# First layer's experts: four weight loads issued in front of the overflow branch, and the first gather of tokens moved behind its own table

## The chip, the cores and the metric

The kernel runs on one core of a Trainium2 chip. The metric is the device time of one execution in microseconds (us). A core has TensorE (PE, matmuls; PEld is its weight load), VectorE (DVE), ScalarE (ACT), GpSimd (POOL) and SyncE (SP), which here issues nearly all loads and stores. Each engine works through its own list of instructions in order and waits on semaphores for the others.

## The reference

Two layers of a diffusion backbone. Each layer modulates and normalises 256 latent and 256 context tokens of width 1024, runs four kinds of attention side by side, and then a mixture of 16 gated experts, of which each token uses two. Cut to the part that matters here:

```python
def _hier_moe(h, wg, bg, we, be, w_gate, w_up, w_down):
    lg = hf @ wg + bg;  grp = argmax(lg)            # one of 4 groups
    le = hf @ we + be                               # 16 experts, the group's 4 are looked at
    top_v, top_i = lax.top_k(le_sel, 2)             # two experts a token
    w_top = softmax(top_v) * p_grp
    for e in range(16):
        a = silu(hf @ w_gate[e]) * (hf @ w_up[e])
        y = y + gate[:, e:e + 1] * (a @ w_down[e])  # 1024 -> 512 -> 1024
```

The first layer does this for all 512 tokens, the second for the 256 latent ones. The weights of one expert are 6 MB in f32, so a layer's experts read 96 MB.

## The kernel before

`moe(l, ...)` first takes the tokens in four chunks of 128 (`for chs, xg, rg, vec in chunks`), routes them and, in the first layer, stores the modulated rows to a DRAM tile `hfD` (lines 1218, 1258 and 1269). It then sorts the tokens' choices, works out a flag (does any expert have more tokens than its slot holds?) and runs `full_experts()` in the first layer and `half_experts()` in the second.

Weights go through a ring of ten buffers of 1 MB (`RING[0]`: two of kind `ra`, eight of kind `rb`). The order of all loads is laid down in `todo`: gate 0 (two loads), then up 0, gate 1, down 0, up 1, gate 2, down 1 and so on, each in two halves. `fetch(n)` issues the next n of them on SP (the issue itself is line 1159, in `load_expert`); `weights()` issues one more whenever a load is used. The constant `FILL` says how many go out where:

```python
FILL = ((4, 1, 1, 0, 1), (10,))     # line 40; first layer, second layer
```

In the first layer four go out when the last chunk begins, one behind each of two stores of `hfD` (line 1218), `FILL[0][3]` of them behind the last store (line 1258), and `FILL[0][4]` at the top of the experts' loop. The rest of the ring is issued inside the first expert, behind its gather; `late=True` puts a one-element memset on GpSimd (line 1158) in front of the first of these. In the second layer all ten go out before the branch.

`overflow()` (lines 1821 and 1822) reads the flag on every engine and skips, by a branch that all five engines take, a block that would treat overflowing experts with loads, gathers and the same buffers. In the skipped case the engines still add to their semaphores, at the join, what the block would have added; on SP these are eight semaphore instructions, one for each counter of loads.

Behind the branch `table(i)` builds expert i's table: one-hots on VectorE (line 1450), small matmuls (line 1452), and the index of its tokens (line 1459). `sort_experts()` sorts the experts by their number of tokens. `start(i)` begins expert i's generator: a gather of 128 rows of `hfD` by GpSimd (line 1490), eight transposes (1500), a copy of their high part by ScalarE (1502) and the low part by VectorE (1503), then the split of each half-load of weights into a high part (ScalarE, line 1472) and a low part (VectorE, in some places GpSimd, line 1474), and three kinds of matmul for each piece (1483, 1484 and 1485; the last one uses the low part of the tokens, line 1503). Down weights go through lines 1533 to 1535. Seven of the 16 experts are small and use the weights directly (lines 1552 to 1596). `tc.issue_after(t[2])` in `start` puts VectorE's instructions of the block it covers behind the instruction that writes the index.

The order on each engine is not the program's: a list scheduler orders the instructions when the kernel is built, by priority in program order and by a simulated clock, except where `issue_after`, `manual_schedule` (SP's loads in the chunk loop) and `keep_in_program_order` hold it.

Of the kernel before, what the change touches and what calls it, by code (L numbers as in the profile page):

```python
# [36 lines left out]
RAW_A = 2  # L37
EB = 6
LOOK = 1
FILL = ((4, 1, 1, 0, 1), (10,))  # L40
AHEAD = 5
STEPS0 = (90, -1, 90, -2, 0, 0, 0, 0, -3, 0, 0, -4, 1, 0, 2, 3, 0, 1, 4, 5, 0, 1)
STEPS1 = (1, 6, 7, 1, 1, 8, 9, 1, 1, 1)
# [54 lines left out]
def kern(tc, I, out):  # L98
# [19 lines left out]
    def nm(s):  # L118
        cnt[0] += 1
        return f"{s}_{cnt[0]}"  # L120
# [28 lines left out]
    start = sp.tile([128, 512], F32, name=nm("amv"), tag="amv", bufs=1)  # L149
# [966 lines left out]
    def moe(l, chunks, mod2):  # L1116
# [20 lines left out]
        ring = RING[l]  # L1137
# [7 lines left out]
        def load_expert(e, n, i, late=False):  # L1145

            x = e if not isinstance(e, int) or e < nfirst else perm[e - nfirst]
            src = I[n][l, x] if isinstance(x, int) else I[n][l, ds(x, 1)].rearrange("a k n -> (a k) n")
            if n == "moe_w_down":
                src, sh = src[256 * i:256 * i + 256], [128, 2, 1024]  # L1150
            else:
                src, sh = src[512 * i:512 * i + 512], [128, 4, 512]
            src = src.rearrange("(p k) n -> p k n", p=128)
            h = sh[1] // 2
            if isinstance(e, int):
                wt = wtile(sh)
                if late:
                    tc.keep_in_program_order(G.memset(wt[0:1, 0, 0:1], 0.0))
                SY.dma_start(wt, src)
                return [wt[:, :h], wt[:, h:]]  # L1160
            ws = []
            for j in range(2):
                wt = tile4([128, h, sh[2]])
                SY.dma_start(wt, src[:, h * j:h * j + h])
                ws.append(wt)
            return ws
# [9 lines left out]
        def small_slot(e):  # L1176

            return isinstance(e, int) and e >= N_FIRST + N_BIG

        def fetch(n, late=False):  # L1180
            for i in range(min(n, len(todo))):
                k = todo.pop(0)
                ahead[k] = load_expert(*k, late and i == 0)
# [7 lines left out]
        def open_ring():  # L1191
            for kind in sorted(set(ring)):
                for i, k in enumerate(ring):
                    if k == kind:
                        first[i] = slot(k, [128, 2, 1024] if todo[i][1] == "moe_w_down" else [128, 4, 512])
# [9 lines left out]
        for chs, xg, rg, vec in chunks:  # L1205
# [4 lines left out]
            if chs[0] == 3:  # L1210
# [4 lines left out]
                loads.__enter__()  # L1215
                fetch(FILL[0][0])
                for store, i in zip(stores, FILL[0][1:]):
                    SY.dma_start(*store)
# [35 lines left out]
            if chs[0] == 3:  # L1254
# [3 lines left out]
                SY.dma_start(hfD[384:512], rg[0])  # L1258
                fetch(FILL[0][3])
                loads.__exit__(None, None, None)  # L1260
# [10 lines left out]
        if half:  # L1271
            PW = Phase(f"pw{l}", "right")
            open_ring()
            fetch(FILL[1][0])
        PX = Phase(f"px{l}")
# [152 lines left out]
        def full_experts():  # L1428
# [58 lines left out]
            def expert(tab, gi, e, xg):  # L1487
# [3 lines left out]
                                     in_offset=bass.IndirectOffsetOnAxis(ap=idx[:, gi, 0:1], axis=0),  # L1491
                                     bounds_check=N - 1, oob_is_err=False)
                if isinstance(e, int) and e == ORDER[0]:

                    fetch(len(ring) - sum(FILL[0]), True)
                Xh, Xl = [PX("t4", [128, KD, 128], F32R, bufs=T4)[:, :, :C] for _ in range(2)]
                for kp in range(2):
                    ps = tr([128, 4, 128])[:, :, :C]
# [110 lines left out]
            def more(e, rk1, rc1):  # L1609
                for _ in expert(tables(lambda i: (rk1, rc1.rearrange("p (c r) -> p c r", r=8)), 1), 0, e, xgs[0]):  # L1610
                    pass
# [4 lines left out]
            def table(i):  # L1616

                s = ORDER[i]
                if s in tabs:
                    return tabs[s]  # L1620
                if s < N_FIRST:
                    tabs[s] = tables(lambda i: (RK[:, :, s], rec[:, :, s]), 1), 0
                    return tabs[s]
                small = small_slot(s)
                end = E if small else N_FIRST + N_BIG
                n = min(3 if s in (N_FIRST, N_FIRST + N_BIG) else 4, end - s)
                rks, recs = sorted_
                t = tables(lambda i: (rks[:, :, s + i], recs[:, :, s + i]), n, small)
                tabs.update((s + i, (t, i)) for i in range(n))
                return tabs[s]  # L1630

            def start(i):
                t, gi = table(i)
                run = (small_expert if small_slot(ORDER[i]) else expert)(t, gi, ORDER[i], xgs[i % 2])
                with tc.issue_after(t[2]):
                    next(run)
                return run

            fetch(FILL[0][4])
            table(0)  # L1640
            table(1)
            rks, gw, E2s = sort_experts()
            recs = R_(E, 8, dt=BF16)
            G.tensor_copy(recs, rec)
            records(recs, E2s, gw)
            sorted_.extend((rks, recs))
            run = start(0)
            next(run)
            for i in range(E):
                if i + 2 < E:  # L1650
# [6 lines left out]
                run = then  # L1657
# [158 lines left out]
        def overflow(cols, more, before=lambda: None):  # L1816
# [5 lines left out]
            with tc.If(fv > 0):  # L1822
# [4 lines left out]
                with tc.For_i(0, E, 1) as e:  # L1827
# [5 lines left out]
                    with tc.For_i(1, N // C, 1):  # L1833
                        V.tensor_scalar(ts[0], ts[0], float(-C), None, op0=ALU.add)
                        more(e, *ts)

        acc = half_experts() if half else full_experts()


# [125 lines left out]
```

## Time and profile before

| what | us |
|---|---|
| three timed runs | 1238.98, 1249.18, 1249.64 |
| their median | 1249.18 |
| the profiled execution | 1250.01 |
| span of its core in the profile | 1248.2 |
| TensorE busy in the span | 1083.0 (87%) |
| VectorE busy in the span | 669.1 (54%) |
| ScalarE busy in the span | 465.0 (37%) |
| queue of the loads, share of the 16 DMA engines | 65.5% |

The span runs from the first to the last instruction of the core; the profiled execution's own time has 1.8 us more around it. All positions in the text are us from the span's start. Shares are averages over stages with different limits, so the stage from 380 us (end of the first layer's routing) to 700 us (end of its experts) is read by itself.

### The profile page before, as it was taken

To read this page: it belongs to the slowest core of one execution; us is meant where nothing else is said; L and a number is where in the kernel's file an instruction comes from. 1 tells how busy PE (TensorE), PEld (TensorE's weight loads), DVE (VectorE), ACT (ScalarE), POOL (GpSimd) and SP (SyncE) were. 2 spreads that over 40 slices of the span, in tenths; PEclk is the share of its full clock that TensorE was granted. 3 is DMA by queue.
4 is the path that set the end of the run, shared out by engine and by line. 5 is a ranking of instruction groups with operands and counts; after the bars stand their busy time and mean duration, and the time that the engine had idled before them with its cause. 6 is when DMAs were issued, how large, how long until landed. Compare 5 with 4: busy or idle time off the path is not lost. (4 is left out here: it accounts for less than half of the span.)

```text
span 1248.2 us, 16457 instructions
## 1 busy us (share of the span) xinstructions
PE 1083.0 (87%) x5930; PEld 689.8 (55%) x5930; DVE 669.1 (54%) x1646; ACT 465.0 (37%) x851; POOL 200.1 (16%) x218
## 2 busy tenths in 40 slices
PE   5999999979961799999989769899989699999973
PEld 2777654457751676666655347654457556565430
DVE  4377166665589795564444478636885721111103
ACT  2342155555252474444434244315563421111100
POOL 0023011212134233132221114120001000000000
PEclk9899989989985799999999978997989789989897
DMA  9843546620634799998997554543714969799995
GB/s 353 312 136 80 198 177 208 237 71 1 245 135 190 244 331 358 412 405 344 416 387 271 204 172 135 148 169 111 270 35 142 406 223 420 322 420 418 377 420 219
DMA packets 85411, 315.83 MB, mean 253 GB/s; under 512 B 20458, under 2 KB 35568, under 8 KB 55624
## 3 DMA queue, kind: packets, MB, share of 16 engines
q1 hardware_dynamic: 81340, 305.99, 65.5%
q0 software_dynamic: 3728, 8.59, 1.9%
q8 instruction: 49, 0.80, 0.3%
q14 instruction: 42, 0.34, 0.1%
q10 hardware_dynamic: 252, 0.09, 0.0%
HBM read 305.47 MB, written 13.70 MB: 256 GB/s over the span
## 5 line engine op out<-in xcount | busy, mean ns | idle before, releaser
L1474 DVE TENSOR_TENSOR hl<-rb,hl 128x1024 fp32r<-128x1024 f32 x71 | 89.1, 1280 | 49.9 <-ACT hl L1472 39.7
L1753 PE MATMUL mm<-rb,xt 128*64 128x256 f32 (+1 forms) x816 | 95.3, 405 | 4.0 <-DMA rb<-in_moe_w_up_dram 4.0
L1472 ACT ACTIVATE hl<-rb 128x1024 fp32r<-128x1024 f32 x84 | 86.1, 1054 | 31.0 <-PE mm L1484 17.6
L579 PE MATMUL mm<-s,hh 128*128 128x512 f32 x216 | 86.8, 406 | 0.0
L581 PE MATMUL mm<-s,hh 128*128 128x512 f32 x216 | 86.6, 404 | 0.0
L580 PE MATMUL mm<-s,hh 128*128 128x512 f32 x216 | 85.8, 397 | 0.0
L1753 PEld LDWEIGHTS mm<-rb,xt 128*64 128x64 f32 (+1 forms) x816 | 50.3, 133 | 39.0 <-issue 12.8
L840 ACT ACTIVATE e<-mm,nmx 128x512 f32<-128x512 f32 (+1 forms) x96 | 58.4, 616 | 29.0 <-DVE nmx L835 14.4
L1483 PE MATMUL mm<-hl,t 128*128 128x512 f32 x144 | 61.1, 424 | 4.0 <-ACT t L1502 4.0
L1485 PE MATMUL mm<-hl,t 128*128 128x512 f32 x144 | 59.2, 414 | 5.2 <-DVE t L1503 5.2
L1484 PE MATMUL mm<-hl,t 128*128 128x512 f32 x144 | 61.5, 427 | 2.3 <-DVE hl L1474 2.3
L835 DVE TENSOR_REDUCE nmx<-mm 128x1 f32<-128x512 f32 (+1 forms) x80 | 52.7, 684 | 7.3 <-PE mm L829 6.3
L849 POOL TENSOR_SCALAR e<-e,rc 128x256 f32<-128x256 f32 x32 | 30.3, 957 | 126.6 <-DVE rc L847 114.7
L440 ACT ACTIVATE s<-ra 128x1024 fp32r<-128x1024 f32 x30 | 31.3, 1055 | 50.5 <-PE mm L581 25.4
L1769 PE MATMUL mx<-rb,at 128*64 128x512 f32 (+1 forms) x192 | 45.6, 598 | 4.6 <-DMA rb<-in_moe_w_down_dram 3.1
L327 PE MATMUL mm<-ra,cT 128*32 128x512 f32 x320 | 46.0, 637 | 3.4 <-DMA ra<-in_w_ada_dram 3.4
L881 PE MATMUL tr<-cst,e 128*128 128x128 f32 x256 | 44.9, 307 | 3.9 <-DVE e L849 1.4
L1758 DVE TENSOR_TENSOR ta<-ta,mm 128x256 f32<-128x256 f32 x13 | 5.5, 420 | 79.9 <-ACT ta L1757 79.9
L579 PEld LDWEIGHTS mm<-s,hh 128*128 128x128 f32 x216 | 40.7, 189 | 12.6 <-issue 2.0
L581 PEld LDWEIGHTS mm<-s,hh 128*128 128x128 f32 x216 | 40.6, 188 | 12.2 <-issue 3.2
L881 PEld LDWEIGHTS tr<-cst,e 128*128 128x128 f32 x256 | 32.0, 154 | 27.1 <-issue 12.8
L580 PEld LDWEIGHTS mm<-s,hh 128*128 128x128 f32 x216 | 40.6, 188 | 11.4 <-issue 2.6
(552 smaller groups left out, 2341.5 us busy)
## 6 DMA issues: line engine op xcount, KB each, us to landing
rb<-in_moe_w_up_dram SPq DMA_DIRECT2D x52, 1024.0 KB
rb<-in_moe_w_down_dram SPq DMA_DIRECT2D x50, 1024.0 KB
rb<-in_moe_w_gate_dram SPq DMA_DIRECT2D x49, 1024.0 KB
ra<-in_w_ada_dram SPq DMA_DIRECT2D x40, 1024.0 KB
ra<-in_moe_w_gate_dram SPq DMA_DIRECT2D x13, 1024.0 KB
ra<-in_w_in_dram SPq DMA_DIRECT2D x24, 512.0 KB
ra<-in_moe_w_down_dram SPq DMA_DIRECT2D x11, 1024.0 KB
ra<-in_moe_w_up_dram SPq DMA_DIRECT2D x10, 1024.0 KB
```

The costliest lines, as they stand in the source:

```text
L579: T.matmul(ps, a, hi[:, k2], start=k == 0, stop=False)
L580: T.matmul(ps, a, lo[:, k2], start=False, stop=False)
L581: T.matmul(ps, b, hi[:, k2], start=False, stop=k == KD - 1)
L835: V.tensor_reduce(nmx[:, :nb], ps, axis=AX, op=ALU.max, negate=True)
L840: S.activation(e[:, b], ps[:, b], AF.Exp, bias=nmx[:, b:b + 1], accum_out=sm[:, b:b + 1])
L881: T.transpose(tp[:, k2, 128 * c:128 * c + 128], probs[hh][c][:, 0, 128 * kt:128 * kt + 128], ident)
L1472: S.activation(hi, w[k2], AF.Copy)
L1474: eng.tensor_tensor(lo, w[k2], hi.bitcast(F32), op=ALU.subtract)
L1483: T.matmul(ps[:C], ah, hs[:, k2], start=first and k2 == 0, stop=False)
L1484: T.matmul(ps[:C], ah, ls[:, k2], start=False, stop=False)
L1485: T.matmul(ps[:C], al, hs[:, k2], start=False, stop=last and k2 == 1)
L1753: T.matmul(ps[o:o + m, j], X[:, k, gi, c:c + m], wt, start=k == 0, stop=k == KD - 1)
```

## The change

The constant becomes `((4, 1, 1, 4), (10,))`: four loads behind the last store of `hfD`, none at the top of the experts' loop and none behind the gather, so that the ring's ten loads all stand before the branch. The first expert's generator now stops (`yield`) right behind its gather. `run = start(0)` moves up, between `table(0)` and `table(1)`; the rest of the first expert (transposes, copies, splits, matmuls) is traced later, by one more `next(run)` at the place where `start(0)` stood, and no longer inside the block of `issue_after`.

```diff
-FILL = ((4, 1, 1, 0, 1), (10,))
+FILL = ((4, 1, 1, 4), (10,))
...
                 if isinstance(e, int) and e == ORDER[0]:
-
-                    fetch(len(ring) - sum(FILL[0]), True)
+                    yield
                 Xh, Xl = [PX("t4", [128, KD, 128], F32R, bufs=T4)[:, :, :C] for _ in range(2)]
...
-            fetch(FILL[0][4])
             table(0)
+            run = start(0)
             table(1)
             rks, gw, E2s = sort_experts()
             recs = R_(E, 8, dt=BF16)
             G.tensor_copy(recs, rec)
             records(recs, E2s, gw)
             sorted_.extend((rks, recs))
-            run = start(0)
+            next(run)
             next(run)
             for i in range(E):
```

## Rows read from the trace of the kernel before

**Rows 1.** Busy time by stretch: us; PE, PEld, DVE, ACT, POOL; clock, DMA share, GB/s.

```profile
394.00:414.00 20.00, 6.40 (x23) 4.41 (x24) 17.94 (x64) 7.33 (x8) 6.99 (x5) 0.50 0.60 228
440.00:697.00 257.00, 241.76 (x1304) 158.96 (x1302) 140.33 (x176) 121.18 (x154) 69.96 (x43) 0.99 0.90 351
```

**Rows 2.** Waits of PE from 440 to 697 us: us in total, times, longest.

```profile
PE mm L1483 <- ACT t L1502: 2.8, 4, 2.0
...
PE mm L1570 <- ACT t L1561: 0.2, 1, 0.2
```

**Rows 3.** Waits of PE from 394 to 440 us.

```profile
PE tr L1500 <- DMA xg<-hfD,idx: 11.0, 1, 11.0
PE mm L1485 <- DVE t L1503: 3.7, 2, 2.3
```

**Rows 4.** Timeline of SP's DMA issues: start, us, engine, line, what, count.

```profile
382.34 0.78 SPq L1159 DMA_DIRECT2D rb<-in_moe_w_down_dram  x1
386.74 0.33 SPq L1258 DMA_DIRECT2D hfD<-r  x1
397.67 0.82 SPq L1159 DMA_DIRECT2D rb<-in_moe_w_up_dram  x2
400.59 0.33 SPq L1159 DMA_DIRECT2D rb<-in_moe_w_down_dram  x1
409.81 0.96 SPq L1159 DMA_DIRECT2D ra<-in_moe_w_gate_dram  x2
```

**Rows 5.** The branch's line, 380 to 400 us: ns min/median/max, first and last start.

```profile
L1822 SPq EVENT_SEMAPHORE  x8: 17/17/17, 396.7 to 397.3; - x8
...
L1822 SPq COMPARE_BRANCH  x1: 54/54/54, 393.6 to 393.6; - x1
```

**Rows 6.** Timeline of ACT, 394 to 413 us; in brackets the idle time before.

```profile
397.31 1.28 ACT L1472 ACT_TABLE_LOAD   x1 [4.95 <-SPq L1822]
398.61 3.90 ACT L1472 ACTIVATE hl<-ra 128x1024 fp32r<-128x1024 f32 x4
...
408.86 0.60 ACT L1502 ACTIVATE t<-tr 128x512 fp32r<-128x512 f32 x1 [5.40 <-PE tr L1500]
```

**Rows 7.** Timeline of DVE, 396 to 413 us.

```profile
398.04 0.22 DVE L1459 TENSOR_SCALAR idx<-tf 128x2 int32<-128x2 f32 x2
399.70 1.23 DVE L1474 TENSOR_TENSOR hl<-ra,hl 128x1024 fp32r<-128x1024 f32 x1 [1.44 <-ACT hl L1472]
...
410.00 0.87 DVE L1450 TENSOR_SCALAR oh<-cst,rt 128x128 bf16<-128x128 f32 x4
...
412.22 0.68 DVE L1503 TENSOR_TENSOR t<-tr,t 128x512 fp32r<-128x512 f32 x1
```

**Rows 8.** The gathers' line, 399 to 400 us and 430 to 435 us.

```profile
L1490 POOL DMA_INDIRECT xg<-hfD,idx x1: 1315/1315/1315, 399.2 to 399.2; - x1
...
DMA to landing us min/median/max: 8.4/8.4/8.4
...
L1490 POOL DMA_INDIRECT xg<-hfD,idx x1: 1014/1014/1014, 431.4 to 431.4; - x1
...
DMA to landing us min/median/max: 4.1/4.1/4.1
```

**Rows 9.** Busy time in stretches of 2 us; the last two columns are DMA share and GB/s.

```profile
386.00:388.00 2.00, 0.00 (x0) 0.00 (x0) 1.97 (x13) 0.21 (x1) 0.00 (x0) 0.50 1.01 410
...
392.00:394.00 2.00, 0.00 (x0) 0.00 (x0) 1.31 (x10) 0.18 (x1) 0.00 (x0) 0.50 0.00 0
...
398.00:400.00 2.00, 0.00 (x0) 0.00 (x0) 0.56 (x4) 1.99 (x3) 0.84 (x1) 0.50 0.55 160
```

**Rows 10.** The branch's line in the second layer, 985 to 1010 us.

```profile
L1822 SPq EVENT_SEMAPHORE  x8: 17/17/17, 1001.9 to 1003.6; - x8
...
L1822 SPq COMPARE_BRANCH  x1: 58/58/58, 995.9 to 995.9; - x1
```

**Rows 11.** Timeline of SP's DMA issues in the second layer, 985 to 1010 us.

```profile
986.32 0.33 SPq L1159 DMA_DIRECT2D rb<-in_moe_w_down_dram  x1
```

**Rows 12.** Busy time in a stretch of 2 us in the second layer, columns as in rows 9.

```profile
1002.00:1004.00 2.00, 2.00 (x9) 1.02 (x9) 1.03 (x5) 0.00 (x0) 0.00 (x0) 0.50 0.04 12
```

## The prediction

> **What bounds the kernel now.** The profiled execution took 1250.01 us, of which 1248.2 us are the span of its core. I read the stage that the change touches in four steps: which engine is busy, what TensorE waits for, what the waited-for engine itself waits for, and where the loads stand meanwhile.
>
> First the busy time by stage. From 440 to 697 us, the experts of the first layer, TensorE is busy 241.8 of 257 us [rows 1]. The load queues are nearly full as well (0.90), so either could be the bound; the waits decide. In those 257 us TensorE waits for other engines 15.1 us in all, spread over eleven reasons from 2.8 down to 0.2 us, and none of them is a weight load [rows 2]. So this stretch is bound by TensorE's own work, and a shift of its start goes through to the end nearly whole. From 394 to 414 us it is the other way round: TensorE is busy 6.4 of 20 us and VectorE 17.9 [rows 1]. This is where the change acts.
>
> There TensorE waits 11.0 us for the first gather, then 3.7 us in two waits for the low half of the gathered tokens (L1503, VectorE) [rows 3]. The first number looks like the prize. It isn't: after the gather TensorE can only run two of its three kinds of products. The third (L1485) needs L1503, which VectorE reaches at 412.22 [rows 7]; between 399.70 and 412.22 VectorE works without a gap on an in-order list that starts with the first low half of a weight (L1474). So the head of the stage is VectorE's list, and that list starts when ScalarE's first high half (L1472) is done.
>
> ScalarE's first work behind the branch is a table load at 397.31, after 4.95 us of idle time that SP's branch line ended [rows 6]. SP compared at 393.6, and its eight semaphore events at the join (L1822) ran from 396.7 to 397.3 [rows 5]. **SP's join at 397.3 is what releases the chain**: join, table load, L1472 at 398.61, L1474 at 399.70, L1503 at 412.22.
>
> **The change, part by part.**
>
> *Loads.* SP's list of before [rows 4] shows what the diff alone doesn't: the seventh load (down weights, 382.34) already went out in front of the branch, even ahead of the last store of tokens (386.74). Behind the branch stood three: two up loads at 397.67 and one down load at 400.59, the latter held by the small memset on GpSimd. The change issues all four behind the store at 386.74, in front of the branch. Four issues cost SP four times 0.33 to 0.41 us [rows 4], at most 1.7 us, so it is done by 388.8, long before it compares at 393.6: nothing there.
>
> When do they land? In the kernel before the queues were empty from 392 to 394 [rows 9]. Without the down load only a store (0.5 MB) and a load (1 MB), both issued before 382.34, go ahead of the last store; at the 410 GB/s of a full row [rows 9] they take 3.8 us, so they are through when it is issued. A flow begins some 1.5 us behind its issue: of the loads issued at 397.67 the row of 398 to 400 holds 0.32 MB, which at 410 GB/s is 0.8 us of transfer [rows 9]. So the store and four loads, 4.7 MB, flow from about 388.3 and need 11.5 us at 410 GB/s: until 399.8 (398.9 with 0.6 us of lag, 400.8 with 2.5 us). Then 2.5 MB are still under way when SP compares at 393.6.
>
> *The join.* In the compiled program of before each of SP's eight events first waits until all loads counted on its counter have landed, then adds what the skipped branch would have counted. At the compare of before everything had landed [rows 9], so these waits cost nothing. The second layer is the nearest row for what comes now: ten loads in front of its branch, the last issued at 986.32 [rows 11], data flowing until 1002 to 1004 [rows 12], compare at 995.9, events from 1001.9 to 1003.6 [rows 10]. The join took 7.7 us there against 3.7 here, and its last event came with the last data. So in the changed kernel the last event comes with or just behind the last load: 400.0 to 401.3, where the upper end is 393.6 plus the 7.7 us. The lower bound of the cost is nothing (if ScalarE's wait concerns only counters without a new load); I take 400.5, that is +3.2 us, as the second layer shows the very case.
>
> Of SP's 3.1 us between compare and first event [rows 5] the Trainium skill has a reason: "Runtime: NRT & Kernel Launch", section Instruction fetch mechanics, says that a taken branch to a page not at hand must wait for a DMA that fetches it. It speaks against this change, as the fetch then shares the engines with the loads; the rows agree so far (3.1 us with empty queues, 6.0 us in the second layer with full ones [rows 10]). By that rule alone the events would run from 399.6 to 400.2 and the join come +2.9 us late, which is the same story 0.3 us cheaper.
>
> *ScalarE and VectorE.* Table load, five high halves, then the copies of the gathered tokens (L1502) stand in one queue. Shifted by 3.2 us the halves run from 401.8 to about 406.6 (0.95 us apart). VectorE's first L1474 moves from 399.70 to 402.9. Everything up to L1503 stands behind it: 12.5 us of work, less what the planner may now put behind L1503. L1503 stood behind eight one-hots of the next table, two rows of 0.87 us [rows 7]; if the tokens are there sooner, these can go behind it: 0 to 1.7 us less. L1503 then starts between 413.7 and 415.4 instead of 412.22: +1.5 to +3.2 us, the middle +2.3.
>
> *The gather.* It starts at 399.2, 0.9 us behind its index (398.26), and lands 8.4 us later beside 3 MB of loads; the one at 431.4, with little beside it, took 4.1 us [rows 8]. Behind its own table alone it can hardly start sooner, as the index ends that wait already. With the loads through at 399.8 it takes 4.1 to 5 us, so the transposes start near 403.9, some 3.7 us sooner than with 8.4 us. But ScalarE is then busy with halves until 406.6; its copies start there instead of at 408.86 [rows 6], 2.3 us sooner, and L1503 waits for VectorE's list anyway. So the 3.7 us are worth nothing beyond the reordering counted above. The removed memset (under 0.1 us on GpSimd) is worth nothing.
>
> *Loads gained.* Three loads land up to 7.7 us sooner. The eleventh goes out at 409.81, when SP has read the sorted experts' numbers, and the next wait for buffers that TensorE's pace frees; TensorE waits for no load up to 697 [rows 2]. Worth nothing.
>
> **Sum.** +2.3 us at L1503, carried whole: 1250.0 + 2.3 = 1252.3 us. Its own range: 0 if the join's wait is partly empty or the two waits for L1503 (2.3 and 1.4 us) [rows 3] absorb it, +4.0 if the join ends at 401.3 and nothing is reordered.
>
> **Rivals.**
>
> *Gain.* The join's events do not hold ScalarE (its counters carry no new load), so L1474 stays at 399.70, and the earlier tokens bring L1503 up by the 1.7 us of one-hots: 1248.3. For it: ScalarE's copies could start 2.3 us sooner. Against it: the second layer's join.
>
> *Slower: the split in front of the index.* Before, VectorE's part of the first expert was traced inside the block that queues it behind the index (issue_after in start). Now that block covers the gather alone. If the planner puts one or two low halves ahead of the index, VectorE stands at 399 with the index and both tables behind a half that waits for ScalarE until 402.9 or 403.8: index at 404.6 to 405.8, gather 0.9 us later, landed at 409.6 to 410.8, which alone puts TensorE's start 2 to 3 us later; VectorE's list behind it (the 14.0 us from index to L1503 less 1.4 us of waiting [rows 7] and the half of 1.2 us that is now ahead: 11.4 us) brings L1503 to 416 to 417.2, +3.8 to +5.0: 1255. It decides as soon as one L1474 stands ahead of L1459.
>
> *Nothing moves.* The gather is ready when its index is, the seventh load was in front already, the join ends unchanged and L1503 keeps its place: 1250.0.
>
> **How the numbers follow.** Forecast (0 to +4 us) 45%; slower through the split 20%; gain 20%; nothing 15%. All four lie within 8 us. About 1% (12.5 us) is what a measurement of this kernel can tell from no change: its own three runs lie between 1238.98 and 1249.64, the median 0.8 us below the profiled execution. So the forecast is 1252. The range must hold the cases (1247 to 1256) and the scatter of a median (a run 10 us lower among three): 1240 to 1259. Faster or slower by over 1% would take a new plan of the instructions far behind the change, which no row excludes and none supports: 4% each.
>
> **What would show it.** In the profile after: four loads behind the store near 387, none from 388 to 409; SP's events at the join ending at 400.0 to 401.3; ScalarE's table load right behind them; the gather landing in 4 to 5 us; transposes near 404, yet L1503 at 413 to 415.5; the stage from 440 as busy as before. Wrong would be: events that end near 397.3 (then the gain), or L1474 ahead of L1459 (then the split).

## The result, and the profile after

The changed kernel takes 1256.76 us (median of 20 runs, 1247.74 to 1260.58) against 1248.55 us for the kernel before (20 runs, 1238.98 to 1252.03). The ratio is 1.0077, interval 1.0061 to 1.0094: 8.2 us slower by the medians, 9.6 us by the ratio. That lies inside the range of the prediction and within 1%, but 4.8 us above its number, which stood for a loss of 2.3 us. In a second set of runs the ratio was 1.009 (1.0058 to 1.0123). The profiled execution of the changed kernel took 1256.33 us, with a span of 1254.5 us. From line 1495 on, line numbers of the changed kernel are those of before minus 1 (L1501 is the old L1502, L1821 the old L1822).

The same views as before, on the changed kernel. Single executions reach the branch at different times (389 to 397 us in this study), so positions are compared by their distance from SP's compare. It is at 393.6 us before and at 392.4 us after.

SP's DMA issues (timeline), to be read against [rows 4]:

```profile
385.53 0.33 SPq L1258 DMA_DIRECT2D hfD<-r  x1
385.91 1.26 SPq L1159 DMA_DIRECT2D rb<-in_moe_w_down_dram  x2
387.21 1.02 SPq L1159 DMA_DIRECT2D rb<-in_moe_w_up_dram  x2
413.99 0.97 SPq L1159 DMA_DIRECT2D ra<-in_moe_w_gate_dram  x2
```

Four loads stand behind the last store and none until 413.99 us. The branch's line, against [rows 5]:

```profile
L1821 SPq EVENT_SEMAPHORE  x8: 17/17/17, 398.4 to 401.1; - x8
...
L1821 SPq COMPARE_BRANCH  x1: 54/54/54, 392.4 to 392.4; - x1
```

The first of the eight events comes 6.0 us behind the compare instead of 3.1, the last one 8.7 instead of 3.7. The timeline of ScalarE, GpSimd and VectorE, against [rows 6 to 8]:

```profile
398.78 1.28 ACT L1472 ACT_TABLE_LOAD   x1 [7.64 <-SPq L1821]
400.08 4.08 ACT L1472 ACTIVATE hl<-ra 128x1024 fp32r<-128x1024 f32 x4
...
415.22 0.60 ACT L1501 ACTIVATE t<-tr 128x512 fp32r<-128x512 f32 x1 [10.11 <-PE tr L1499]
...
404.29 3.30 POOL L1474 TENSOR_TENSOR hl<-ra,hl 128x1024 fp32r<-128x1024 f32 x1 [10.31 <-DVE hl L1474]
409.52 1.31 POOL L1490 DMA_INDIRECT xg<-hfD,idx  x1 [1.93 <-DVE idx L1459]
...
395.15 0.41 DVE L1376 TENSOR_TENSOR t<-rk 128x256 f32<-128x256 f32 x1
401.16 1.23 DVE L1474 TENSOR_TENSOR hl<-ra,hl 128x1024 fp32r<-128x1024 f32 x1 [5.60 <-ACT hl L1472]
...
403.04 2.35 DVE L1474 TENSOR_TENSOR hl<-ra,hl 128x1024 fp32r<-128x1024 f32 x2
...
405.45 2.42 DVE L1388 TENSOR_TENSOR t<-rk,cst 1x256 f32<-1x256 f32 x1
...
407.93 1.21 DVE L1474 TENSOR_TENSOR hl<-rb,hl 128x1024 fp32r<-128x1024 f32 x1
409.07 0.22 DVE L1459 TENSOR_SCALAR idx<-tf 128x2 int32<-128x2 f32 x2
...
415.85 0.69 DVE L1502 TENSOR_TENSOR t<-tr,t 128x512 fp32r<-128x512 f32 x1 [0.85 <-ACT t L1501]
```

This is the picture of the second rival. VectorE stands idle for 5.60 us because a low half (L1474) is now ahead of the index (L1459) and waits for ScalarE, which waits for the late join. Four low halves are ahead of the index in all. The index comes at 409.07 instead of 398.04 us, the gather at 409.52 instead of 399.2, and L1502 at 415.85 instead of 412.22. The gather itself now lands in 4.2 us instead of 8.4, which helps nobody.

Waits of TensorE from 394 to 440 us, against [rows 3], and busy time, against [rows 1]:

```profile
PE tr L1499 <- DVE rt L1417: 18.6, 1, 18.6
PE tr L1452 <- DVE oh L1450: 0.4, 1, 0.4
PE mm L1483 <- ACT t L1501: 0.3, 1, 0.3
```

```profile
394.00:414.00 20.00, 1.31 (x7) 0.73 (x7) 14.21 (x53) 6.24 (x6) 5.64 (x3) 0.50 0.29 108
...
440.00:697.00 257.00, 237.52 (x1277) 156.63 (x1278) 139.31 (x178) 119.98 (x152) 70.61 (x42) 0.99 0.91 353
```

One wait of 18.6 us takes the place of several. The 3.7 us of [rows 3] are not one place: in TensorE's timeline of the kernel before, 1.38 us of them belong to the first expert and 2.35 us to the second one, 17 us later, where 1.27 us for the high part of its tokens stand in front:

```profile
412.96 0.79 PE L1485 MATMUL mm<-hl,t 128*128 128x512 f32 x1 [1.38 <-DVE t L1503]
...
426.94 0.50 PE L1483 MATMUL mm<-hl,t 128*128 128x512 f32 x1 [1.27 <-ACT t L1502]
...
430.45 0.79 PE L1485 MATMUL mm<-hl,t 128*128 128x512 f32 x1 [2.35 <-DVE t L1503]
```

That second L1503 stands in VectorE's list of before behind one-hots of the third table and a low half:

```profile
426.51 1.95 DVE L1450 TENSOR_SCALAR oh<-cst,rt 128x128 bf16<-128x128 f32 x3
...
428.39 1.21 DVE L1474 TENSOR_TENSOR hl<-rb,hl 128x1024 fp32r<-128x1024 f32 x1
...
429.72 0.68 DVE L1503 TENSOR_TENSOR t<-tr,t 128x512 fp32r<-128x512 f32 x1
```

In the changed kernel the second stop is gone (0.3 us are left of it), and by 436 us most of the loss has disappeared. Two rows of busy time (us; PE, PEld, DVE, ACT, POOL; granted clock, DMA share, GB/s) show it, first of the kernel before, then of the changed one:

```profile
428.00:432.00 4.00, 1.65 (x5) 1.26 (x5) 3.33 (x10) 0.60 (x1) 0.57 (x1) 0.76 0.81 283
432.00:436.00 4.00, 4.00 (x18) 3.33 (x17) 0.70 (x1) 2.60 (x3) 2.84 (x2) 0.81 0.42 121
```

```profile
428.00:432.00 4.00, 3.71 (x23) 2.65 (x22) 3.69 (x9) 3.44 (x5) 2.47 (x1) 1.00 0.80 279
432.00:436.00 4.00, 4.00 (x20) 3.10 (x19) 4.00 (x8) 3.09 (x4) 2.79 (x1) 1.00 0.88 313
```

Before, after those stops, TensorE's granted clock fell from 1.00 (2.4 GHz) to 0.76 and 0.81, a mix of both levels. After, it works through at 1.00: VectorE did most of the sort and the one-hots of the second table while TensorE waited for the first gather.

All kernels of the study in one table. The times are read from their timelines: SP's compare, then the distances from it to the first L1485, to the 9th scatter and to the 15th (a scatter is the DMA by which GpSimd writes one expert's finished rows to `yD`). Behind them stands the time between these two, worked from the unrounded times. In the variants the line numbers shift by up to four; the column L1485 is the same product everywhere.

```
                            compare  L1485  9th    15th   9th-15th  median    ratio (interval)
before                      393.60   19.4   194.2  303.1  108.9     -         1
before again                392.20   19.9   195.2  304.2  109.0     -         -
changed                     392.38   25.4   195.5  308.0  112.5     1256.76   1.0077 (1.0061-1.0094)
r_after                     395.67   25.4   195.7  308.0  112.3     1260.01   1.009  (1.0058-1.0123)
e1_hold                     392.60   17.5   195.8  305.8  110.0     1252.68   1.005  (1.0031-1.007)
e2_order_only               392.66   22.7   198.4  309.7  111.2     1255.18   1.0057 (1.0028-1.0086)
e4_early                    392.97   15.4   193.7  306.0  112.3     1247.63   0.9999 (0.9975-1.0023)
n2_sort_first               392.70   19.5   194.3  306.4  112.1     1249.13   1.0024 (0.9995-1.0054)
s1_second_behind_sort       396.98   13.0   191.4  303.9  112.5     1251.02   1.0036 (1.0007-1.0065)
s2_split_behind_sort        392.83   15.4   188.2  296.9  108.8     1241.68   0.9968 (0.9942-0.9993)
r_s2                        396.22   15.6   188.0  296.7  108.8     1243.65   0.9972 (0.9955-0.9988)
s3_change_and_sort          389.61   15.4   191.2  305.6  114.4     1248.47   1.0014 (0.9994-1.0034)
s4_old_loads_sort           392.25   17.6   191.6  301.7  110.2     1245.87   1.0004 (0.9978-1.0029)
```

Three programs have two profiles each; between compare and 9th or 15th scatter they repeat within 1.1 us (the kernel before itself stands at 194.2 and 195.2 at the 9th), the stretch between 9th and 15th within 0.2 us.

### The profile page after: what moved, and what is told of

It reads as the page before. It is cut to its first block, busy times and chain, and to the rows that moved or that the text cites. A ratio compares the mean times of both kernels' runs of the same rounds, so it can differ in the third digit from the quotient of the medians.

```text
span 1254.5 us, 16457 instructions
## 1 busy us (share of the span) xinstructions
PE 1078.8 (86%) x5930; PEld 686.2 (55%) x5930; DVE 668.5 (53%) x1646; ACT 464.8 (37%) x851; POOL 201.5 (16%) x217
## 5 line engine op out<-in xcount | busy, mean ns | idle before, releaser
L1474 DVE TENSOR_TENSOR hl<-rb,hl 128x1024 fp32r<-128x1024 f32 x71 | 90.5, 1302 | 41.1 <-ACT hl L1472 27.3
L1752 PE MATMUL mm<-rb,xt 128*64 128x256 f32 (+1 forms) x816 | 92.4, 387 | 4.7 <-DMA rb<-in_moe_w_up_dram 4.7
L1472 ACT ACTIVATE hl<-rb 128x1024 fp32r<-128x1024 f32 x84 | 85.8, 1055 | 24.1 <-PE mm L1533 11.5
L1485 PE MATMUL mm<-hl,t 128*128 128x512 f32 x144 | 58.4, 408 | 1.4 <-DVE t L1502 1.4
L581 PEld LDWEIGHTS mm<-s,hh 128*128 128x128 f32 x216 | 40.6, 188 | 12.3 <-issue 3.2
```

Of the source, the lines that this page charges most:

```text
L581: T.matmul(ps, b, hi[:, k2], start=False, stop=k == KD - 1)
L1472: S.activation(hi, w[k2], AF.Copy)
L1474: eng.tensor_tensor(lo, w[k2], hi.bitcast(F32), op=ALU.subtract)
L1485: T.matmul(ps[:C], al, hs[:, k2], start=False, stop=last and k2 == 1)
L1752: T.matmul(ps[o:o + m, j], X[:, k, gi, c:c + m], wt, start=k == 0, stop=k == KD - 1)
```

## The experiments

**The two parts apart.** `e2_order_only` keeps the loads of before and moves only the gather:

```diff
 (kernel before)
+                    yield                  # behind the late fetch in expert()
...
             table(0)
+            run = start(0)
             table(1)
...
-            run = start(0)
+            next(run)
             next(run)
```

> The other half of the change alone: the first gather behind its own table and the rest of the first expert no longer queued behind the index, but the loads as in the kernel before (seven in front of the branch, three behind it). Theory 'split': the gather starts 8 to 10 us late as in the changed kernel, time 1254 to 1257, ratio 1.005 to 1.008. Theory 'join': SP's events end at 397.3 as before and there is no loss: 1248.5, ratio 1.000. Theory 'plan': anything, as the later order differs from both kernels.

Measured: 1255.18 us, ratio 1.0057. The join is as before (events 2.9 to 3.5 us behind the compare), but four low halves stand ahead of the index, which comes 13.9 us behind the compare instead of 4.4. The first L1485 comes 3.4 us later, and here the stage keeps it (9th scatter 4.2 us later). One load moves after all: the last of the three behind the branch, held by the memset behind the gather, goes out at 408.5 us. So moving the split out of the block that queues it behind the index costs by itself.

`e1_hold` keeps the change and puts the block back around the split; the order of all instructions is then that of the new `FILL` alone:

```diff
 (changed kernel)
-            next(run)
+            with tc.issue_after(tabs[ORDER[0]][0][2]):
+                next(run)
             next(run)
```

> The changed kernel, but VectorE's part of the first expert is again queued behind the index (issue_after around its first continuation); loads stay in front of the branch. VectorE's list then has the index of both tables ahead of the first low half, as in the kernel before. Theory 'split' (the loss is the low halves that stand ahead of the index): the gather starts at 399 to 401 instead of 409.5 and the loss of 8 us goes, all but the late join: 1249 to 1252, ratio to the kernel before 1.000 to 1.003. Theory 'join' (the loss is SP's late join with loads in flight): the table load of ScalarE stays 2.7 us late and the loss stays, 1256, ratio 1.006. Theory 'plan' (the loss is the other order of the later experts, not the head of the stage): the head recovers, but the time stays near 1254.

Measured: 1252.68 us, ratio 1.005. The index is back at 4.4 us behind the compare; the join stays late (events 5.6 to 8.8 us behind it). The time lies above what 'split' expected (1.000 to 1.003). The first L1485 comes 1.8 us sooner than before, yet the 9th scatter 1.6 us later (0.6 against the kernel before again). TensorE's waits from 394 to 440 us say why:

```profile
PE tr L1499 <- DVE tf L1460: 7.1, 1, 7.1
PE tr L1452 <- DVE rt L1433: 5.3, 1, 5.3
```

The second line is new: TensorE has done the first expert's gate and stands before the product of the third table (L1452), which needs the sort's records (L1433) on VectorE. In this order low halves are planned ahead of the records, so these end at 427 us; in the kernel before they ended at 414 us. A head that comes sooner is waited away one step later.

`r_after` is the changed kernel again.

> The changed kernel once more, for a second profile and on the same chip as its variants: ratio 1.006 to 1.009. If the stretch from 435 to 590 again stands within 1.5 us of the kernel before and the rest of the loss arises behind it, the head's delay is regained there and the loss has a second place.

Measured: 1260.01 us, ratio 1.009, and the same distances as the first time.

`e4_early` has the structure of before, but loads that go out early enough to land before the branch:

```diff
 (kernel before)
-FILL = ((4, 1, 1, 0, 1), (10,))
+FILL = ((4, 4, 2, 0), (10,))
...
-                if isinstance(e, int) and e == ORDER[0]:
-
-                    fetch(len(ring) - sum(FILL[0]), True)
...
-            fetch(FILL[0][4])
```

> The kernel before with all ten loads in front of the branch, but early: four at the start of the last chunk, four behind the first store, two behind the second, none behind the last (FILL 4, 4, 2, 0); no gather moved. They have landed at about 390, before SP compares at 393. Theory 'join': the events end 3.7 us behind the compare as in the kernel before, and the gather lands in 4 us instead of 8.4 since no load runs beside it; the time is that of the kernel before or up to 2 us better, 1246.5 to 1248.5, ratio 0.998 to 1.000. If instead loads in front of the branch cost by being there at all (buffers, SP's list, the later order): 1250 to 1252.

Measured: 1247.63 us, ratio 0.9999. Events 3.5 to 4.1 us behind the compare, first L1485 4.0 us sooner than before, 9th scatter only 0.5 us sooner, 15th 2.9 us later.

**What makes the join late.** `j2_beside` is `e4_early` with two copies of 2 MB from DRAM to DRAM on GpSimd's queue behind the last store. They are under way at the compare, but no counter of SP's join waits for them.

```diff
 (e4_early)
                 loads.__exit__(None, None, None)
+                if not half:
+                    beside = tc.dram_tile([2 * N, D], F32, name="beside")
+                    for i in range(2):
+                        G.dma_start(beside[N * i:N * i + N], hfD)
                 continue
```

> Early loads and the order of the kernel before, with two copies of 2 MB from DRAM to DRAM added on GpSimd's queue behind the last store: they are under way when SP compares, but no counter of SP's join waits for them. Theory (two parts make the join late: SP's instructions behind the taken branch are fetched by DMA and that waits beside other transfers, and the last two events wait for their loads to land): the first of SP's eight events comes 4.5 to 6.5 us behind the compare, the eighth within 0.7 us of the first, and ScalarE's table load right behind. Rival (the events only wait for loads to land): first event 3.1 to 3.6 us behind the compare, as without the copies (3.5). The copies delay GpSimd's own join and the first gather, so the total is not compared.

Its branch line:

```profile
L1822 SPq EVENT_SEMAPHORE  x8: 17/17/17, 396.8 to 397.4; - x8
...
L1822 SPq COMPARE_BRANCH  x1: 54/54/54, 391.2 to 391.2; - x1
```

The first event comes 5.6 us behind the compare with nothing to wait for (from 392 to 396 us SP's load queue moves no packet, the copies move 1.90 MB), and the others follow within 0.6 us. ScalarE's table load starts 6.0 us behind the compare. So the first part of the delay is not a wait for loads to land. It goes with the packets of instructions. From 394 to 396 us, in the kernel before and in the changed one (DMA view: queue, kind, packets, MB, share of 16 engines):

```profile
q14 instruction: 3, 0.02, 4.9%
q8 instruction: 1, 0.02, 3.0%
```

```profile
q1 hardware_dynamic: 115, 0.85, 100.7%
q14 instruction: 1, 0.01, 1.0%
```

Before, four instruction packets are through within 2.4 us of the compare, on queues that carry nothing else. After, with the loads filling the engines, only one of them has begun by 396 us, 3.6 us behind the compare; the other three begin from 396 to 398 us. In `j2_beside`, beside the copies, the first begins 3.9 us behind the compare, against 0.9 in the kernel before. The spread of the eight events is the second part. In the changed kernel they take 2.7 us from first to last, in `j2_beside` and before 0.5 to 0.6 us. In the compiled program the seventh event waits on the counter of the last load, and the eighth stands behind it: in the changed kernel the load's last part landed at 401.06 us and the event came at 401.08.

**The sort in front of the split.** If the sort's records are the second chain, they should go first. `s2_split_behind_sort` has the early loads of `e4_early`, the order of the changed kernel, and puts everything of the first expert behind the last record:

```diff
 (changed kernel, FILL = ((4, 4, 2, 0), (10,)))
-            records(recs, E2s, gw)
+            done = records(recs, E2s, gw)      # returns its last instruction
             sorted_.extend((rks, recs))
-            next(run)
-            next(run)
+            with tc.issue_after(done):
+                next(run)
+                next(run)
```

> As the run before it, but all halves of the first expert and the low part of its tokens stand behind the records of the sort. Theory (two chains, the later one counts): the first L1485 comes 2 to 5 us later than with the first two halves in front (411 to 414 against 408.4), no stop at the third table behind it, first scatter within 1.5 us of the run before it, total 1244 to 1249. Rival (the head's shift is carried whole): first scatter and total 2 to 5 us later than in the run before it.

Measured: 1241.68 us, ratio 0.9968 (0.9942 to 0.9993), faster than both kernels. Its VectorE timeline:

```profile
397.27 0.22 DVE L1460 TENSOR_SCALAR idx<-tf 128x2 int32<-128x2 f32 x2
...
404.02 0.31 DVE L1433 CAST rt<-rt 128x64 bf16<-128x64 f32 x1
404.92 0.69 DVE L1503 TENSOR_TENSOR t<-tr,t 128x512 fp32r<-128x512 f32 x1 [0.59 <-ACT t L1502]
...
406.38 1.22 DVE L1475 TENSOR_TENSOR hl<-ra,hl 128x1024 fp32r<-128x1024 f32 x1
```

The whole sort fits between index and tokens, while VectorE would have waited for ScalarE. The records end at 404.3 us, 11.5 us behind the compare (20.5 before), and L1503 comes 12.1 us behind it (18.6 before). The first L1485 comes as soon as in `e4_early` (15.4 us behind the compare in both), not the 2 to 5 us later that I had expected; against `s1_second_behind_sort` (shown below; the "run before it" of the expectation) it is 2.4 us later. The first scatter comes 2.1 us sooner than there, behind the compare, where I had expected it within 1.5, and the total lies below the expected 1244. The stop at the third table did not go: TensorE still waits 2.6 us for its one-hots near 430 us. From 394 to 440 us TensorE is then busy 34.12 us, against 28.78 before (first row: before, second: `s2_split_behind_sort`):

```profile
394.00:440.00 46.00, 28.78 (x130) 22.30 (x131) 37.00 (x104) 24.19 (x27) 12.86 (x8) 0.72 0.70 248
```

```profile
394.00:440.00 46.00, 34.12 (x158) 26.01 (x159) 44.95 (x116) 28.12 (x32) 14.69 (x8) 0.78 0.60 211
```

That is 5.3 us more, 4.6 with the compare 0.8 us sooner taken off, and the 9th scatter comes 6.0 us sooner. The run was repeated as `r_s2`:

> The fastest version so far once more (early loads, all halves of the first expert behind the records of the sort; 1241.7 us, ratio 0.9968 with an interval from 0.9942 to 0.9993). If the gain belongs to the order, the ratio is again 0.994 to 0.999 and the scatters from 520 to 590 us stand again some 6 us sooner behind the compare than before. If it was a chance of one chip, the ratio is 0.999 to 1.003.

Measured: 1243.65 us, ratio 0.9972 (0.9955 to 0.9988), the same distances within 0.2 us.

`s1_second_behind_sort` leaves the first two halves in front and puts only the next ones behind the records:

```diff
 (s2_split_behind_sort)
-            with tc.issue_after(done):
+            with tc.issue_after(tabs[ORDER[0]][0][2]):
                 next(run)
+            with tc.issue_after(done):
                 next(run)
```

> All ten loads go out early enough to have landed before the branch (four when the last chunk begins, four and two behind the first two stores), the first gather stands behind its own table, the first two halves of weights behind the index, and the next ones behind the records of the sort. Theory (up to 435 us the stage is gated by the later of two chains on VectorE, the head and the sort with the third table; a head that comes sooner is only waited away at the table's product L1452): records done near 410, no stop of TensorE over 1 us from 418 to 432, first scatter 440 to 443 against 444.3 with the same loads and the old order, total 1243 to 1248. Rival (the head's shift is carried whole): the halves that are held back delay the first expert by 1 to 4 us, first scatter 445 to 448, total 1248 to 1252.

Measured: 1251.02 us, ratio 1.0036: a miss in the total. It has the earliest first L1485 of all, 13.0 us behind the compare, and the 9th scatter comes 3.2 us later than in `s2_split_behind_sort`. TensorE again stands at the third table, 3.4 and 3.2 us in two waits (414 to 440 us); the expected end of these stops did not come. The records were done at 416.3 us, not near 410.

`s3_change_and_sort` and `s4_old_loads_sort` are `s2_split_behind_sort` with other loads: those of the change, and those of before.

```diff
 (s2_split_behind_sort)
-FILL = ((4, 4, 2, 0), (10,))
+FILL = ((4, 1, 1, 4), (10,))               # s3
+FILL = ((4, 1, 1, 0, 1), (10,))            # s4, with both fetch() of before
```

> The change exactly as it is (four loads behind the last store, the first gather right behind its own table), with one thing added: the low part of the tokens and all halves of the first expert stand behind the records of the sort on VectorE. Theory (the join is late by 2.7 us, but VectorE now needs nothing from ScalarE before the records are done, so the late join is hidden; and the sort is no longer the later chain): events and ScalarE's table load as late as with the change alone (6 us behind the compare), first L1485 15 to 18 us behind the compare against 25.4 with the change alone and 19.4 before, total 1240 to 1246. Rival (a late join is carried whole by whatever comes next): first L1485 18 us or more behind the compare, total 1246 to 1251.

Measured: 1248.47 us, ratio 1.0014: the head as expected, the total not. The join is as late as with the change (5.4 to 8.4 us behind the compare), and yet the first L1485 comes 15.4 us behind the compare, as with early loads. VectorE needs nothing of ScalarE until the records are done, so the late join is covered. At the 9th scatter the kernel is 3.0 us ahead of before; between 9th and 15th it loses 5.5 us (114.4 against 108.9).

> The loads of before (one in front of the branch, three behind it beside the gather), the gather right behind its own table, and the low part of the tokens and all halves of the first expert behind the records of the sort. Theory (the sort's place in VectorE's list is what gains; the loads only set when the tokens land): gather lands 8 us after its start instead of 4, first L1485 17 to 20 us behind the compare, total 1243 to 1248, so most of the gain of the early loads with the same order (1241.7) is the order's. Rival (the early loads make the gain): total 1247 to 1252, as before or slower.

Measured: 1245.87 us, ratio 1.0004. The first L1485 comes 17.6 us behind the compare, the 9th scatter 2.6 us sooner than before. The order alone gains nearly as much up to there as with the loads of the change. The total lies where the theory had it, but so does the kernel before in the same set (1246.35): at the 15th scatter 1.4 us of the gain are left. The early loads with this order (`s2_split_behind_sort`) are 3.4 us further ahead at the 9th scatter, so more of that gain comes with the loads than the theory said.

**Behind the stage.** `n2_sort_first` is the kernel before with one exchange in the program's order:

```diff
 (kernel before)
             table(0)
-            table(1)
             rks, gw, E2s = sort_experts()
+            table(1)
```

> The kernel before with one exchange in the program's order: the sort is traced ahead of the second table. Loads and gather stay as before. TensorE's order is the one of before up to the later experts and then differs in the places in which it differs with the changed loads. Theory (the loss from 590 us on comes from a new plan of later instructions, not from loads or gather): stage as before up to 590 us within 1 us, then 1 to 3 us lost up to the end of the experts, total 1248 to 1252. Rival (the loss from 590 us on comes from the loads' timing): nothing lost from 590 to 700 us (within 0.5), total 1246 to 1248.5.

Measured: 1249.13 us, ratio 1.0024 (0.9995 to 1.0054). The 9th and the 15th scatter on GpSimd (timeline), kernel before and `n2_sort_first`:

```profile
587.80 1.57 POOL L1541 DMA_INDIRECT yD<-t,idx  x1 [12.88 <-ACT hl L1472]
...
696.70 0.97 POOL L1541 DMA_INDIRECT yD<-t,idx  x1 [7.62 <-DVE t L1540]
```

```profile
587.03 1.24 POOL L1541 DMA_INDIRECT yD<-t,idx  x1 [12.86 <-ACT hl L1472]
...
699.13 0.98 POOL L1541 DMA_INDIRECT yD<-t,idx  x1 [7.65 <-DVE t L1540]
```

Head and stage are those of before (194.3 against 194.2 us behind the compare), loads and gather are untouched, and still 3.2 us are lost between the two scatters. TensorE's instructions differ from those of before in a few places up to there, in the same later experts as in `e1_hold` and `e4_early`.

What is lost there has two parts, TensorE's waits and its busy time between the two scatters. The waits are 9.9 us before, 11.7 in `n2_sort_first` and 12.3 in the changed kernel; the busy time is 99.1, 100.5 and 99.9 us. The waits go with the order of instructions. `e1_hold` and `s2_split_behind_sort` have one order in this stretch on all five engines, and both wait 9.9 us. `s3_change_and_sort` and `s4_old_loads_sort`, whose loads differ, have one order but for a high half on ScalarE (behind a small expert's copy, L1595, in the first, ahead of it in the second), and they wait 13.9 and 12.2 us. The busy time does not go with the order: it is 100.1 and 98.9 us in the first pair (granted clock 0.97 and 0.98), 100.5 and 98.0 us in the second (0.97 and 1.00). So of the changed kernel's 3.6 us, 2.4 are waits that come with another order, and the rest is mostly busy time. Its order differs from that of before in many more places than the order of `n2_sort_first`, and no run shows which of them costs the waits.

`r_before`, the kernel before again, tells whether this is scatter:

> The kernel before once more, for its own profile. If the loss of the changed kernel behind 590 us belongs to the changed kernel, this profile repeats the first one of before: the same distances between the scatters from 440 to 697 us within 0.5 us, and a granted clock of 1.00 from 915 to 945 us. If it is scatter of single executions, they differ here by 1 to 4 us.

Measured: 109.0 against 108.9 us, so it isn't. Its clock from 915 to 945 us was 0.94, against 1.00 in the first profile and 0.84 and 0.83 in the two of the changed kernel.

## Why the prediction came out as it did

The time lies in the stated range, but that is luck: the range was wide for the scatter of a median, and the mechanism that the forecast of +2.3 us stood for did not come. The 1255 of the second rival is close by luck too, as its delay was to be carried whole and wasn't.

- **What bounds the head: right.** Join, table load, L1472, L1474 in VectorE's list is the chain, and the change made the join late. One reading of it was wrong: of the "two waits for L1503" only 1.38 us are the head's, the 2.35 us are the second expert's, at 430 us.
- **Loads: right in the main.** Four issues near 387 us, then none until 414; from 400 to 402 us the DMA share is down to 0.02. The issues took 2.3 us, not at most 1.7, which cost nothing, and the last load landed 8.7 us behind the compare instead of 6.2.
- **Join: size near, cause wrong.** Predicted +3.2 us for ScalarE's table load; measured +2.7 (6.4 us behind the compare instead of 3.7). I put it all on the wait for loads to land. Six of the eight events came together, 2.9 us late, and `j2_beside` shows that delay with nothing to land. The wait for landing exists, but it held the last two events alone, behind the table load. That it did not hold ScalarE was luck: before, ScalarE's last wait ended right behind the seventh event (397.21 us, table load 397.31), in the changed program right behind the fourth (398.69, table load 398.78); the seventh came at 401.08. The late first events are what the Trainium skill says in "Runtime: NRT & Kernel Launch", section Instruction fetch mechanics: a taken branch whose target is not at hand must wait for a DMA fetch. The trace agrees, with +2.9 us on the first event as the prediction worked it out for that rule.
- **VectorE's list: the step that failed.** The forecast took the index to stay ahead of the halves. They were planned ahead of it, four of them, and the second rival came: index 16.7 us behind the compare instead of 4.4, L1502 4.8 us later by that measure, inside the +3.8 to +5.0 us of the rival. `e2_order_only` shows it without the loads, `e1_hold` without the split.
- **"Carried whole": wrong, in both directions.** The waits from 440 us on were too few to absorb a delay, but a second chain was hidden ahead of 440 us: VectorE's list behind the head, with the sort's records, the third table and the second expert's tokens. Before, TensorE stopped again for these tokens from 425 to 431 us (1.27 and 2.35 us) and its clock fell. The first L1485 of the changed kernel is 6.0 us later, the 9th scatter 1.3 us (0.3 against the kernel before again). With `e1_hold`, where the records stop TensorE for 5.3 us, the first L1485 is 1.8 us sooner and the scatter no sooner. I had read the rows of 394 to 440 us as one head, and never asked what would be late next if it moved.
- **Gather and removed memset: right**, worth nothing.
- **A loss far behind the change, through a new plan: named at 4%, and a loss came, at a smaller size.** Between 9th and 15th scatter the changed kernel loses 3.6 us, repeated within 0.2 us; TensorE's waits there are 12.3 us instead of 9.9. `n2_sort_first` loses 3.2 us there without any change of loads or gather. Of the nine programs other than before in the table (the changed one is one of them) eight are 1.1 to 5.5 us slower there, and one is level (108.8). Of the 3.6 us, 2.4 are waits, which follow the order of instructions in the two pairs above; the rest doesn't follow it, so the new plan is the cause of the larger part and not shown for all of it.

The sum by distances: 0.3 to 1.5 us up to the 9th scatter, by which profiles are compared, and some 3.5 more up to the 15th, of some 8 in the medians. The rest, about 3 us, arises behind the experts: from the 15th scatter to the end of the span 554.2 and 554.7 us in the changed kernel, 551.5 and 551.8 before. In both profiles of the changed kernel the clock is lower from 915 to 945 us. But `s2_split_behind_sort` and its repetition differ by 4 us in that stretch with one program (555.7 and 551.6), so what makes these 3 us stays open.

## What to carry to other kernels

Before a transfer is moved in front of a branch, look at what is in flight when the engines take it: their next instructions come over the same DMA engines, and here that made SP's first events 2.9 us late at 2.5 MB in flight, and cost nothing up to the first L1485 once the first work behind the join no longer needed the late engine (`s3_change_and_sort`). When an engine with an in-order list is the head of a stage, hold the order that matters (index, then sort, then split) explicitly, as an edit that only moves code can let the scheduler undo it. A delay in a stage with two chains isn't carried as it is: price the chain that is next. And reckon with a few us far behind the change in a 1250 us kernel: here 0 to 5.5 between two scatters 200 us later.

## What was not expected of the hardware

Small instructions on VectorE took the time of a large one on GpSimd. In the kernel before (timeline, GpSimd then VectorE), and without GpSimd beside it in `s2_split_behind_sort`:

```profile
402.65 3.94 POOL L1474 TENSOR_TENSOR hl<-ra,hl 128x1024 fp32r<-128x1024 f32 x1 [0.84 <-issue]
...
404.31 2.30 DVE L1392 CAST pi<-pf 1x16 int32<-1x16 f32 x1
```

```profile
398.61 0.15 DVE L1392 CAST pi<-pf 1x16 int32<-1x16 f32 x1
```

A cast of 16 numbers took 2.30 us and ended with GpSimd's instruction (402.65 + 3.94 = 406.59; 404.31 + 2.30 = 406.61); alone it took 0.15. In the changed kernel L1388 took 2.42 us beside GpSimd's L1474. The Trainium skill, "SBUF — State Buffer", section SBUF: two separate sides, says that VectorE (in a two-port mode, or with two inputs in SBUF) and GpSimd share one pair of ports under an exclusive lock, and that the loser waits for the whole instruction. These rows agree as to the wait; by which of the two conditions the cast takes the lock, no run here shows. Having the sort done before GpSimd's first half spares the sort this stall, but doesn't remove it: in `s2_split_behind_sort` one-hots pay, beside GpSimd's L1475 (408.72 us, 2.85 us long); five take 3.22 us where four took 0.87:

```profile
409.23 3.22 DVE L1451 TENSOR_SCALAR oh<-cst,rt 128x128 bf16<-128x128 f32 x5
```
